# A Strassen-type down-projection reordered, with raw weights loaded by quadrants, the last norm on VectorE, and gate weights of two precisions in one tile

## Chip, cores and metric

One Trainium2 chip, one core. The metric is the time on the device of one launch, in microseconds. The kernel before takes 1428.85 us (median of three runs, 1427.64 to 1430.25).

## The reference

One layer of a hybrid decoder in float32: 1024 prompt tokens and 64 sample tokens (1088 rows together), width 1024. A norm, one input projection, a retention group and an mLSTM group, an output projection with norm and residual, then a feed-forward part with a causal convolution. What matters here, cut:

```
gates = h @ w_in[:, last 8 columns] + b_g         # input and forget gate of 4 heads
...
up   = rmsnorm(x, pre_ffn_g) @ w_up                # 1024 -> 2 * 2816
conv = sum(padded[:, j:j+L] * conv_w[j] for j in range(3)) + conv_b
ffn  = (gelu(conv[..., :2816]) * conv[..., 2816:]) @ w_down      # 2816 -> 1024
x    = x + rmsnorm(ffn, post_ffn_g)
```

## The kernel before

Activations lie transposed, features on partitions, tokens in four blocks of Q = 272 columns. A float32 product is made of three fp32r matmuls: both operands are split into a high part (a ScalarE copy) and a low part (a VectorE subtraction), and high x high, high x low, low x high are summed in PSUM. The program's instructions are ordered per engine by a scheduler ahead of time; an instruction that is ready in its model may stand in a queue before one that comes earlier in the code. `tc.issue_after` puts an instruction behind a given one of the same engine.

The gate projection (`gate_proj`, L281) uses one padded weight tile in which 4 of the first 32 columns are forget gates and 4 of the next 32 are input gates; `dense` (L153) makes 8 x 3 matmuls for each of four blocks, and two VectorE products with `rb` take the result from PSUM (L303, L304).

The down-projection is one level of a Strassen-Winograd scheme: seven products (`SEQ`, L1035) in place of eight, each over KH = 11 pairs of 128 input features, on 512 weight columns and 544 tokens. Weight quadrants A11, A21 are the two halves of one 512 KB row block of `w_down`, A12 and A22 those of the next; GpSimd forms S1 to S4 from them in place (L1074, tile `wd`). The matching activation operands B11 ... T4 were written to HBM (`bd`) by the up-projection and are loaded again per step (tile `rb`, L1083). `prep` (L1076) makes one step: load, split of the weight (`ra`, L1053 and L1054), split of the activations. `ready` keeps eight steps ahead of TensorE. A raw weight tile takes the place of an up-projection operand, so its loads wait for that operand's last matmul.

`mm` (L1111, tile `dn`) issues three matmuls of 272 columns; eight PSUM banks hold a product's 2 x 4 outputs. `evac` (L1136) adds them to four output blocks `facc`, two halves of four slices each; `sumsq` (L1126) squares a finished slice (ScalarE), adds it to the block's sum (VectorE, tile `facc_sq`) and applies the gain (ScalarE). In the last product, S4 x B22, the two token halves follow each other, 132 matmuls each, and between them the finished blocks are normed: `norm_rows` sums over partitions with a matmul by ones (L185) and makes the reciprocal root (L186 to L191), `write` multiplies (L1194), adds the residual `x1r` (L1195) and stores. The block sums of squares that are still missing at the start of that product are made in its second step (`half_square`).

```
todo = {0: lambda: [load_x1(b) for b in range(2)], 1: lambda: (half_square(), load_x1(2), load_x1(3)),
        3: lambda: norm_rows(0), 4: lambda: write(0), 5: lambda: norm_rows(1)}
...
todo = {0: lambda: write(1), 2: lambda: (norm_rows(2), write(2)), 3: lambda: (norm_rows(3), write(3))}
```

The first set stands behind the steps of the first half, the second behind the four groups of 33 matmuls of the second half.

Of the kernel before, what the change touches and what calls it, by code (L numbers as in the profile page):

```python
# [16 lines left out]
P = 128  # L17
# [75 lines left out]
def hybrid_layer_kernel(ctx: ExitStack, tc: tile.TileContext, a: dict, o: dict):  # L93
# [86 lines left out]
    def rstd_block(ssq, out, l, r, name, after=None):  # L180

        n = out.shape[1]
        ps = bank(psB, n, f"ssqb_{name}")
        with tc.issue_after(after.ins) if after else nullcontext():
            nc.tensor.matmul(ps, ones, ssq, start=True, stop=True)  # L185
        nc.vector.tensor_scalar(out, ps, 1.0 / D, EPS, ALU.mult, ALU.add)  # L186
        nc.scalar.activation(l, ps, AF.Ln, scale=1.0 / D, bias=eps)
        nc.scalar.activation(r, l, AF.Exp, scale=-0.5)
        nc.scalar.activation(l, r, AF.Square)
        nc.vector.scalar_tensor_tensor(l, l, -0.5, out, ALU.mult, ALU.mult)  # L190
        nc.vector.scalar_tensor_tensor(out, l, 1.5, r, ALU.add, ALU.mult)  # L191
# [92 lines left out]
    def gate_proj():  # L284
        xst = m2.tile([P, X_SEL], F32, tag="vx", bufs=1, name="xst")
        nc.sync.dma_start(xst, a["cx"][:, :X_SEL])
        xsel = m2.tile([P, X_N - X_SEL], F32, tag="sb", bufs=1, name="xsel")
        nc.sync.dma_start(xsel, a["cx"][:, X_SEL:])
        nc.vector.tensor_copy(idb, ident)
        nc.vector.tensor_copy(negb, xst[:, X_NEG:X_NEG + P])  # L290
        for t in vts:
            nc.gpsimd.memset(t[:, :, P:P + 1], 1.0)
        nc.vector.tensor_copy(negsb, xst[:, X_NEGS:X_NEGS + TS])
        nc.scalar.activation(sel, xsel[:100, :].rearrange("p (j h c) -> p j h c", j=2, h=NH), AF.Copy)
        fg = tok("fg", NH)
        ig = yT[3][:NH, 0, :]
        gates.extend([fg, ig])
        w = load_w(a["wg"], "gates")
        for b in range(4):
            o0, n = BLK[b]  # L300
            ps = bank(psA, n, f"gates{b}")
            dense(ps, w, h, b)
            nc.vector.tensor_tensor(fg[:, o0:o0 + n], ps[0:NH, :], rb[0:NH, o0:o0 + n], ALU.mult)  # L303
            nc.vector.tensor_tensor(ig[:, o0:o0 + n], ps[32:32 + NH, :], rb[32:32 + NH, o0:o0 + n], ALU.mult)  # L304
        nc.scalar.activation(fg, fg, AF.Identity, bias=vec[0:NH, V_BG:V_BG + 1])
        nc.scalar.activation(ig, ig, AF.Identity, bias=vec[0:NH, V_BG + 1:V_BG + 2])

# [724 lines left out]

    nc.sync.dma_start(o["conv"], cache.rearrange("p j s t -> p (j s t)"))
    log_exp_tables(last["gelu"])
    SEQ = (("A11", "B11"), ("A12", "B21"), ("A22", "T4"), ("S2", "T2"), ("S1", "T1"), ("S3", "T3"), ("S4", "B22"))  # L1035

    PLACE = {"A11": 0, "A21": 512, "A12": 1024, "A22": 1536, "S1": 0, "S3": 512, "S4": 1024, "S2": 1536}
# [13 lines left out]
    def halves(x, hi, lo):  # L1051
# [3 lines left out]
        return hi, lo  # L1055

    A, B, late = {}, {}, []
    sums_of = {1: ("S3", "A11", "A21", ALU.subtract), 2: ("S2", "A22", "S3", ALU.subtract),
               3: ("S1", "S2", "A11", ALU.add), 4: ("S4", "A12", "S2", ALU.subtract)}

    def prep_a(q, p):
        name = SEQ[q][0]
        if q < 2:
            nc.sync.dma_start(raw[p][:, q * D:(q + 1) * D], a["wd"][2 * p + q])
        if q == LAST and p > 7:
            if p % 2 == 0:
                late.append(slot(SLOTS[len(late)], f"ra_late{p}").rearrange("p k n -> p (k n)"))
            t = late[-1][:, p % 2 * D:(p % 2 + 1) * D]
        else:
            t = ring_a[(q * KH + p) % 8]  # L1070
        A[q, p] = halves(quad(p, name), t[:, :512], t[:, 512:])
        if q in sums_of:
            out, x, y, op = sums_of[q]
            nc.gpsimd.tensor_tensor(quad(p, out), quad(p, x), quad(p, y), op)  # L1074

    def prep(n):  # L1076

        q, p = divmod(n, KH) if n < LAST * KH else (LAST, 0)
        t = ring_b[n % 8]
        hi, lo = t[:, :HB], t[:, HB:]  # L1080
        if q < LAST:
            o0 = BD[SEQ[q][1]]
            nc.sync.dma_start(lo.bitcast(F32), bd[p][:, o0:o0 + HB])  # L1083
            prep_a(q, p)
            B[q, p] = halves(lo.bitcast(F32), hi, lo)
            return
        i, p = divmod(n - LAST * KH, 6)
        ps = range(2 * p, min(2 * p + 2, KH))
        o0 = BD["B22"] + i * Q
# [33 lines left out]
    acc = [t_acc[b // 2][:, b % 2 * Q:(b % 2 + 1) * Q] for b in range(4)]  # L1123
    begun = set()

    def sumsq(b, m, final=None):  # L1126

        t = facc[b][:, m, :]
        sq = acc[b] if b not in begun else t_acc[b // 2][:, 2 * Q:]
        nc.scalar.activation(sq, t, AF.Square)  # L1130
        if b in begun:
            nc.vector.tensor_tensor(acc[b], acc[b], sq, ALU.add)  # L1132
        begun.add(b)
        nc.scalar.activation(t, t, AF.Copy, scale=vec[:, V_POSTFFN + m:V_POSTFFN + m + 1])
# [161 lines left out]
```

## Time and profile before

| | |
|---|---|
| median of three runs | 1428.85 us |
| the profiled execution | 1428.44 us, span 1426.7 us |
| TensorE busy | 1361.6 us, 95% |
| VectorE busy | 1060.2 us, 74% |
| ScalarE busy | 587.0 us, 41% |
| GpSimd busy | 436.4 us, 31% |
| read from HBM, written | 97.88 MB, 35.50 MB |
| first down-projection matmul, last one | starts at 1152.27, at 1407.85 |

Times of rows are from the start of the span. Matmuls are pipelined, so a busy TensorE isn't one at its peak: look at the distance of starts, and at the granted clock. An idle stretch is put down to what released it.

### The profile page before, as it was taken

The page shows a single profiled execution, that of the slowest core. Times are in us where ns is not written, and L with a number is a line of the kernel's source. Part 1 is how long each engine was busy: PE and PEld are TensorE (multiplying, and loading weights), DVE is VectorE, ACT ScalarE, POOL GpSimd, SP SyncE. Part 2 cuts the span into 40 slices and gives each one's busy share as a digit, 9 for nine tenths or more (in the row PEclk, how much of TensorE's full clock was granted, in tenths as well). Part 3 has the DMA queues.
Part 4 walks back from the last instruction along what each step waited for, and adds up shares of the span by engine and source line. Part 5 has one row for each costly group of instructions (what it writes and reads, how often), then busy time and mean ns, then how long its engine had stood idle before and what let it go on. Part 6 is the DMA issues. An engine that isn't in the chain of part 4 may idle for free. (4 is left out here: it accounts for less than half of the span.)

```text
span 1426.7 us, 26779 instructions
## 1 busy us (share of the span) xinstructions
PE 1361.6 (95%) x10575; PEld 1332.3 (93%) x10575; DVE 1060.2 (74%) x2064; ACT 587.0 (41%) x1162; POOL 436.4 (31%) x433
## 2 busy tenths in 40 slices
PE   7999999999999999999998999999999979999993
PEld 7899999999999998999998999999999979999993
DVE  7845875455455466568899999999989995995577
ACT  6423542323223236445553433433433444454462
POOL 5200000001001000004456466465465460952015
PEclk9999999999999999999999999999999989999997
DMA  6112111121121113323022223322223394333352
GB/s 233 60 45 73 41 59 54 53 62 48 45 62 47 45 47 112 113 63 122 32 92 87 89 88 112 107 85 84 99 85 115 116 404 121 95 91 93 97 197 114
DMA packets 64478, 135.12 MB, mean 95 GB/s; under 512 B 6112, under 2 KB 30688, under 8 KB 63840
## 3 DMA queue, kind: packets, MB, share of 16 engines
q1 hardware_dynamic: 64352, 133.41, 27.6%
q8 instruction: 83, 1.36, 0.4%
q14 instruction: 43, 0.35, 0.1%
HBM read 97.88 MB, written 35.50 MB: 93 GB/s over the span
## 5 line engine op out<-in xcount | busy, mean ns | idle before, releaser
L159 PE MATMUL in<-hh,wh_in 128*128 128x272 f32 x1024 | 301.8, 295 | 11.1 <-ACT hh L198 6.8
L161 PE MATMUL in<-hh,wl_in 128*128 128x272 f32 x1024 | 301.1, 294 | 1.1 <-DVE wl_in L147 1.1
L160 PE MATMUL in<-hl,wh_in 128*128 128x272 f32 x1024 | 299.8, 293 | 1.2 <-DVE hl L199 1.2
L159 PEld LDWEIGHTS in<-hh,wh_in 128*128 128x128 f32 x1024 | 195.4, 191 | 12.9 <-ACT hh L198 6.8
L161 PEld LDWEIGHTS in<-hh,wl_in 128*128 128x128 f32 x1024 | 194.9, 190 | 3.7 <-issue 2.1
L160 PEld LDWEIGHTS in<-hl,wh_in 128*128 128x128 f32 x1024 | 195.4, 191 | 2.4 <-DVE hl L199 1.5
L147 DVE TENSOR_TENSOR wl_up<-st_up,wh_up 128x512 fp32r<-128x512 f32 x128 | 125.4, 985 | 9.5 <-ACT wh_up L145 9.4
L145 ACT ACTIVATE wh_up<-st_up 128x512 fp32r<-128x512 f32 x128 | 75.1, 620 | 133.1 <-POOL st_up L866 120.4
L1054 DVE TENSOR_TENSOR rb<-rb 128x544 fp32r<-128x544 f32 x78 | 73.1, 949 | 42.4 <-ACT rb L1053 42.2
L943 DVE SCALAR_TENSOR_TENSOR c<-Ug,vec,c 128x1024 f32<-128x1024 f32 x88 | 79.4, 939 | 9.5 <-ACT c L941 9.5
L1074 POOL TENSOR_TENSOR wd<-wd 128x512 f32<-128x512 f32 x44 | 72.0, 1667 | 42.7 <-DVE ra_dhi L1054 33.1
L943 DVE SCALAR_TENSOR_TENSOR c<-Uv,vec,c 128x1024 f32<-128x1024 f32 (+1 forms) x88 | 71.9, 822 | 9.3 <-ACT c L941 9.3
L958 POOL TENSOR_TENSOR act<-act 128x544 f32<-128x544 f32 x44 | 72.4, 1645 | 14.7 <-DVE act L950 10.3
L1053 ACT ACTIVATE rb<-rb 128x544 fp32r<-128x544 f32 x78 | 49.8, 648 | 64.3 <-DMA rb<-bd 58.4
L613 POOL TENSOR_TENSOR vx_r<-vts,cst 64x1024 f32<-64x1024 f32 x4 | 7.6, 1901 | 191.8 <-ACT vts L527 191.8
L902 DVE TENSOR_TENSOR Uv<-Uv,up_S 128x272 f32<-128x272 f32 (+1 forms) x200 | 63.5, 369 | 0.0
L941 ACT ACTIVATE c<-Ug,vec 128x1024 f32<-128x1024 f32 (+1 forms) x44 | 34.6, 835 | 67.0 <-DVE Ug L906 59.3
L145 ACT ACTIVATE wh_in<-st_in 128x1024 fp32r<-128x1024 f32 x32 | 33.9, 1059 | 62.3 <-PE in L160 58.3
L893 POOL MEMSET Ug<- 128x2 f32 x22 | 2.2, 100 | 176.9 <-DVE xr L791 82.1
L859 POOL TENSOR_TENSOR s<-st_up 128x512 f32<-128x512 f32 x20 | 29.0, 1450 | 85.2 <-DMA st_up<-in_wu 82.1
L613 POOL TENSOR_TENSOR vx_m<-vts,cst 64x1032 f32<-64x1032 f32 x4 | 7.7, 1914 | 152.6 <-DVE pt_m L559 152.6
L928 PE MATMUL up_A<-T4h,wh_up 128*128 128x272 f32 x160 | 47.9, 299 | 4.8 <-DVE Uv L902 4.7
(547 smaller groups left out, 4825.1 us busy)
## 6 DMA issues: line engine op xcount, KB each, us to landing
st_up<-in_wu SPq DMA_DIRECT2D x44, 512.0 KB, 3.3
rb<-bd SPq DMA_DIRECT2D x76, 272.0 KB, 2.8
bd<-act SPq DMA_DIRECT2D x33, 544.0 KB, 2.7
st_in<-in_wi SPq DMA_DIRECT2D x32, 512.0 KB, 3.3
wd<-in_wd SPq DMA_DIRECT2D x22, 512.0 KB, 9.3
x<-in_x SPq DMA_DIRECT2D x16, 272.0 KB, 7.0
xr<-in_x SPq DMA_DIRECT2D x8, 544.0 KB, 3.7
x1d<-mo SPq DMA_DIRECT2D x8, 544.0 KB, 3.1
```

The costliest lines, as they stand in the source:

```text
L145: nc.scalar.activation(hi, x, AF.Copy)
L147: eng.tensor_tensor(lo, x, hi.bitcast(F32), ALU.subtract)
L159: nc.tensor.matmul(ps, hi[:, ws], xh, start=k == 0, stop=False)
L160: nc.tensor.matmul(ps, hi[:, ws], xl, start=False, stop=False)
L161: nc.tensor.matmul(ps, lo[:, ws], xh, start=False, stop=k == KT - 1)
L902: nc.vector.tensor_tensor(o_, o_ if x is None else c(x), c(ps), ALU.add)
L928: nc.tensor.matmul(ps, wh[:, c], xh[:, k, n], start=k == 0, stop=False)
L943: nc.vector.scalar_tensor_tensor(c, u(i), cw(i), c, ALU.mult, ALU.add)
L958: nc.gpsimd.tensor_tensor(o_, x, y, ALU.subtract)
L1053: nc.scalar.activation(hi, x, AF.Copy)
L1054: nc.vector.tensor_tensor(lo, x, hi.bitcast(F32), ALU.subtract)
L1074: nc.gpsimd.tensor_tensor(quad(p, out), quad(p, x), quad(p, y), op)
```

## The change

The gate weights' high and low parts are put side by side in one tile of 128 columns, so two matmuls (by the high and the low activations) give four partial products; the lower 64 rows of PSUM are copied by ScalarE and added to the upper 64 by VectorE. In the down-projection, product A22 x T4 moves from third to last, S3, S2, S1 follow earlier in that order, and the sums S are formed in the step that uses them (S2 now in the place of S3). Raw weights are loaded as four quadrants of 256 KB: A11, A12, A22 with products 0, 1, 2, and A21 from the seventh step on. With A22 x T4 last, the first half of that product completes block 0 and the second block 1; blocks 2 and 3 are complete before it. The final multiplication and addition of `write` run on VectorE alone. The last square of block 1 isn't added to the sum: a second ones matmul adds it in PSUM. The last block is written in 4, 3 and 1 slices.

```diff
@@ rstd_block
-            nc.tensor.matmul(ps, ones, ssq, start=True, stop=True)
+            for i, x in enumerate(ssq if type(ssq) is list else [ssq]):
+                nc.tensor.matmul(ps, ones, x, start=i == 0, stop=type(ssq) is not list or i == len(ssq) - 1)
@@ gate_proj
-        w = load_w(a["wg"], "gates")
+        st = stage_w(a["wg"], "gates").rearrange("p (k c) -> p k c", k=KT)
+        w = wp.tile([P, D], F32R, tag="whi", name="w_gates").rearrange("p (k c) -> p k c", k=KT)
+        split_to(st[:, :, :64], w[:, :, :64], w[:, :, 64:])
...
-            dense(ps, w, h, b)
-            nc.vector.tensor_tensor(fg[:, o0:o0 + n], ps[0:NH, :], rb[0:NH, o0:o0 + n], ALU.mult)
-            nc.vector.tensor_tensor(ig[:, o0:o0 + n], ps[32:32 + NH, :], rb[32:32 + NH, o0:o0 + n], ALU.mult)
+            for k in range(KT):
+                for i, x in enumerate(h[b // 2][k // 4]):
+                    nc.tensor.matmul(ps, w[:, k, :], x[:, k % 4, qcols(b)], start=k == i == 0,
+                                     stop=k == KT - 1 and i == 1)
+            gs = m2.tile([P, Q], F32, tag="sw", name=f"gs{b}")[:64, :n]
+            nc.scalar.activation(gs, ps[64:, :], AF.Copy)
+            nc.vector.tensor_tensor(gs, gs, ps[:64, :], ALU.add)
+            nc.vector.tensor_tensor(fg[:, o0:o0 + n], gs[0:NH, :], rb[0:NH, o0:o0 + n], ALU.mult)
+            nc.vector.tensor_tensor(ig[:, o0:o0 + n], gs[32:32 + NH, :], rb[32:32 + NH, o0:o0 + n], ALU.mult)
@@ down-projection
-    SEQ = (("A11", "B11"), ("A12", "B21"), ("A22", "T4"), ("S2", "T2"), ("S1", "T1"), ("S3", "T3"), ("S4", "B22"))
+    SEQ = (("A11", "B11"), ("A12", "B21"), ("S3", "T3"), ("S2", "T2"), ("S1", "T1"), ("S4", "B22"), ("A22", "T4"))
-    PLACE = {..., "S1": 0, "S3": 512, "S4": 1024, "S2": 1536}
+    PLACE = {..., "S1": 0, "S3": 512, "S4": 1024, "S2": 512}
-    sums_of = {1: ("S3", ...), 2: ("S2", ...), 3: ("S1", ...), 4: ("S4", ...)}
+    sums_of = {2: ("S3", ...), 3: ("S2", ...), 4: ("S1", ...), 5: ("S4", ...)}
+    def load_quad(name, p):
+        c = PLACE[name] % D
+        nc.sync.dma_start(quad(p, name), a["wd"][2 * p + PLACE[name] // D, :, c:c + 512])
@@ prep_a
-        if q < 2:
-            nc.sync.dma_start(raw[p][:, q * D:(q + 1) * D], a["wd"][2 * p + q])
+        if q < 3:
+            load_quad(("A11", "A12", "A22")[q], p)
+        if 0 <= q * KH + p - 6 < KH:
+            load_quad("A21", q * KH + p - 6)
+        if q in sums_of:                          # moved up from behind the split
+            out, x, y, op = sums_of[q]
+            nc.gpsimd.tensor_tensor(quad(p, out), quad(p, x), quad(p, y), op)
@@ sumsq
-        if b in begun:
+        if apart:
+            acc[b] = [acc[b], sq]
+        elif b in begun:
             nc.vector.tensor_tensor(acc[b], acc[b], sq, ALU.add)
@@ evac
-        o_, x = ((c11, c22), None, (c22, c22), (c12, c22), (c22, c12), (c12, c12))[q - 1]
+        o_, x = ((c11, c22), None, (c22, c22), (c12, c22), (c12, c12), (c21, c21))[q - 1]
...
+        if q == 4:
+            nc.vector.tensor_tensor(c22, c21, t, ALU.add)
+            sumsq(2 + i, 4 + m)
         if q == 5:
-            nc.vector.tensor_tensor(c21, c21, t, ALU.add)
-            sumsq(i, 4 + m)
+            sumsq(2 + i, m)
         if q == 6:
-            sumsq(2 + i, m)
+            sumsq(i, 4 + m, (i, m) == (1, 3))
@@ write
-        for k0, k1 in ((0, 3), (3, 6), (6, 8)):
+        for k0, k1 in ((0, 4), (4, 7), (7, 8)) if b == 1 else ((0, 3), (3, 6), (6, 8)):
             t = facc[b][:, k0:k1, :]
-            mul = nc.gpsimd if b == 3 and k0 == 6 else nc.vector
-            add = nc.vector if b == 3 and k0 < 6 else nc.gpsimd
-            mul.tensor_tensor(t, t, r.unsqueeze(1).broadcast_to([P, k1 - k0, n]), ALU.mult)
-            add.tensor_tensor(t, t, x1[b][:, k0:k1, :], ALU.add)
+            nc.vector.tensor_tensor(t, t, r.unsqueeze(1).broadcast_to([P, k1 - k0, n]), ALU.mult)
+            nc.vector.tensor_tensor(t, t, x1[b][:, k0:k1, :], ALU.add)
             nc.sync.dma_start(yo[:, k0:k1, :], t)
@@ last product, first half, then second half
-    todo = {0: lambda: [load_x1(b) for b in range(2)], 1: lambda: (half_square(), load_x1(2), load_x1(3)),
-            3: lambda: norm_rows(0), 4: lambda: write(0), 5: lambda: norm_rows(1)}
+    todo = {0: lambda: [load_x1(b) for b in (2, 3, 0, 1)], 2: lambda: norm_rows(2), 3: lambda: write(2),
+            4: lambda: norm_rows(3)}
...
-    todo = {0: lambda: write(1), 2: lambda: (norm_rows(2), write(2)), 3: lambda: (norm_rows(3), write(3))}
+    todo = {0: lambda: write(3), 1: lambda: norm_rows(0), 2: lambda: write(0), 3: lambda: (norm_rows(1), write(1))}
```

## Rows read from the trace of the kernel before

**Rows 1.** Busy time by stretch: PE, PEld, DVE, ACT, POOL; clock, DMA share, GB/s
```profile
100.00:200.00 100.00, 96.98 (x739) 92.10 (x739) 71.81 (x195) 43.24 (x87) 4.96 (x5) 0.98 0.17 53
```

**Rows 2.** The same, at the start of the down-projection:
```profile
1155.00:1160.00 5.00, 2.99 (x15) 2.67 (x15) 5.00 (x8) 1.27 (x3) 4.21 (x5) 0.72 1.03 414
```

**Rows 3.** Timeline of product 0: start, duration, line; idle before and releaser in brackets
```profile
1152.27 0.29 PE L1118 MATMUL dn<-rb,ra_whi 128*128 128x272 f32 x1
...
1199.10 0.40 ACT L1140 ACTIVATE facc<-dn 128x272 f32<-128x272 f32 x1 [0.36 <-PE dn L1120]
```

**Rows 4.** Timeline of TensorE, fifteen dn matmuls in a row, first and last:
```profile
1381.33 0.29 PE L1118 MATMUL dn<-rb,ra_late 128*128 128x272 f32 x1
...
1383.08 0.29 PE L1120 MATMUL dn<-rb,ra_late 128*128 128x272 f32 x1
```

**Rows 5.** TensorE's waits, 1130 to 1250: total us, times, longest
```profile
PE dn L1118 <- DVE Uv L902: 4.4, 3, 2.6
PE dn L1118 <- ACT rb L1053: 2.2, 1, 2.2
...
PE dn L1119 <- DVE rb L1054: 1.5, 1, 1.5
```

**Rows 6.** Timeline of TensorE at the end of the last product:
```profile
1395.92 0.29 PE L1120 MATMUL dn<-rb,ra_late 128*128 128x272 f32 x1
1400.69 1.27 PE L185 MATMUL ssqb_fin<-facc_sq,ones 128*128 128x272 f32 x2 [4.48 <-DVE facc_sq L1132]
1401.37 0.81 PE L1118 MATMUL dn<-rb,ra_whi 128*128 128x272 f32 x1
...
1407.85 0.29 PE L1120 MATMUL dn<-rb,ra_late 128*128 128x272 f32 x1
```

**Rows 7.** Busy time by stretch, the last 33 dn matmuls:
```profile
1401.30:1408.20 6.90, 6.84 (x35) 6.50 (x33) 5.03 (x9) 3.30 (x8) 1.13 (x2) 0.63 0.25 94
```

**Rows 8.** Timeline of VectorE at the end:
```profile
1406.45 4.27 DVE L1194 TENSOR_TENSOR facc<-facc,fin 128x816 f32<-128x816 f32 x3
1410.65 0.42 DVE L1143 TENSOR_TENSOR facc<-facc,dn 128x272 f32<-128x272 f32 x1
1411.57 1.23 DVE L1132 TENSOR_TENSOR facc_sq<-facc_sq 128x272 f32<-128x272 f32 x1 [0.49 <-ACT facc_sq L1130]
...
1416.70 3.06 DVE L1194 TENSOR_TENSOR facc<-facc,fin 128x816 f32<-128x816 f32 x2
1419.68 3.05 DVE L1195 TENSOR_TENSOR facc<-facc,x1r 128x816 f32<-128x816 f32 x2
```

**Rows 9.** VectorE by line: duration in ns, least, median, most:
```profile
L1132 DVE TENSOR_TENSOR facc_sq<-facc_sq x28: 426/438/2174, 1235.5 to 1411.6; 128x272 f32<-128x272 f32 x28
L1143 DVE TENSOR_TENSOR facc<-facc,dn x40: 422/427/439, 1232.1 to 1410.7; 128x272 f32<-128x272 f32 x40
L1195 DVE TENSOR_TENSOR facc<-facc,x1r x2: 995/1562/2129, 1419.7 to 1421.7; 128x816 f32<-128x816 f32 x2
L1054 DVE TENSOR_TENSOR rb<-rb x78: 430/725/1871, 1139.2 to 1381.2; 128x544 fp32r<-128x544 f32 x76, 128x272 fp32r<-128x272 f32 x2
```

**Rows 10.** The gates' tile, one of its three matmul groups:
```profile
L161 PE MATMUL gates<-hh,wl_gates x32: 282/288/391, 122.5 to 143.6; 128*128 128x272 f32 x32
```

**Rows 11.** The raw weights' tile, its load issues:
```profile
L1064 SPq DMA_DIRECT2D wd<-in_wd x22: 327/332/806, 1137.5 to 1164.2; - x22
```

**Rows 12.** Timeline of SP's queue, two groups of issues:
```profile
1151.28 8.18 SPq L1064 DMA_DIRECT2D wd<-in_wd  x8
1160.41 1.56 SPq L1083 DMA_DIRECT2D rb<-bd  x2
```

**Rows 13.** Tile rb, its loads:
```profile
DMA to landing us min/median/max: 2.0/2.8/9.2
```

**Rows 14.** DMA issues of the page: KB each, median us to landing
```profile
st_up<-in_wu SPq DMA_DIRECT2D x44, 512.0 KB, 3.3
```

**Rows 15.** Busy time by stretch, loads of x at the kernel's start:
```profile
10.00:14.00 4.00, 4.00 (x20) 4.00 (x20) 4.00 (x8) 3.81 (x9) 1.72 (x3) 1.00 1.03 412
```

More of the change, by code (lines that the diff above doesn't have):

```diff
@@ L1034, in hybrid_layer_kernel @@
     log_exp_tables(last["gelu"])
-    SEQ = (("A11", "B11"), ("A12", "B21"), ("A22", "T4"), ("S2", "T2"), ("S1", "T1"), ("S3", "T3"), ("S4", "B22"))
-    PLACE = {"A11": 0, "A21": 512, "A12": 1024, "A22": 1536, "S1": 0, "S3": 512, "S4": 1024, "S2": 1536}
+    SEQ = (("A11", "B11"), ("A12", "B21"), ("S3", "T3"), ("S2", "T2"), ("S1", "T1"), ("S4", "B22"), ("A22", "T4"))
+    PLACE = {"A11": 0, "A21": 512, "A12": 1024, "A22": 1536, "S1": 0, "S3": 512, "S4": 1024, "S2": 512}
     LAST = len(SEQ) - 1
@@ L1057, in hybrid_layer_kernel @@
     A, B, late = {}, {}, []
-    sums_of = {1: ("S3", "A11", "A21", ALU.subtract), 2: ("S2", "A22", "S3", ALU.subtract),
-               3: ("S1", "S2", "A11", ALU.add), 4: ("S4", "A12", "S2", ALU.subtract)}
+    sums_of = {2: ("S3", "A11", "A21", ALU.subtract), 3: ("S2", "A22", "S3", ALU.subtract),
+               4: ("S1", "S2", "A11", ALU.add), 5: ("S4", "A12", "S2", ALU.subtract)}
+    def load_quad(name, p):
+        c = PLACE[name] % D
+        nc.sync.dma_start(quad(p, name), a["wd"][2 * p + PLACE[name] // D, :, c:c + 512])
     def prep_a(q, p):
         name = SEQ[q][0]
-        if q < 2:
-            nc.sync.dma_start(raw[p][:, q * D:(q + 1) * D], a["wd"][2 * p + q])
+        if q < 3:
[5 more added lines that the diff above has]
+            nc.gpsimd.tensor_tensor(quad(p, out), quad(p, x), quad(p, y), op)
         if q == LAST and p > 7:
@@ L1071, in prep_a @@
         A[q, p] = halves(quad(p, name), t[:, :512], t[:, 512:])
-        if q in sums_of:
-            out, x, y, op = sums_of[q]
-            nc.gpsimd.tensor_tensor(quad(p, out), quad(p, x), quad(p, y), op)
     def prep(n):
@@ L1088, in prep @@
         ps = range(2 * p, min(2 * p + 2, KH))
-        o0 = BD["B22"] + i * Q
+        o0 = BD[SEQ[LAST][1]] + i * Q
         m = len(ps) * Q
@@ L1124, in hybrid_layer_kernel, with sumsq @@
     begun = set()
-    def sumsq(b, m, final=None):
+    def sumsq(b, m, apart=False):
         t = facc[b][:, m, :]
@@ L1139, in evac @@
         if q in (0, 2):
-            nc.scalar.activation((c22, c11, c21)[q], t, AF.Copy)
+            nc.scalar.activation((c22, None, c21)[q], t, AF.Copy)
             return
-        o_, x = ((c11, c22), None, (c22, c22), (c12, c22), (c22, c12), (c12, c12))[q - 1]
+        o_, x = ((c11, c22), None, (c22, c22), (c12, c22), (c12, c12), (c21, c21))[q - 1]
         nc.vector.tensor_tensor(o_, x, t, ALU.add)
@@ L1170, in hybrid_layer_kernel @@
             ready((q + 1) * KH + 2)
-    x1, fin = [], []
+    x1, fin = {}, {}
     def load_x1(b):
-        x1.append(slot(SLOTS[2 + b], f"x1r_{b}", F32).rearrange("p k n -> p (k n)").rearrange("p (k n) -> p k n", k=KT))
+        x1[b] = slot(SLOTS[2 + b], f"x1r_{b}", F32).rearrange("p k n -> p (k n)").rearrange("p (k n) -> p k n", k=KT)
         nc.sync.dma_start(x1[b], x1cols(b))
@@ L1179, in load_x1 @@
             t = slot(SLOTS[6 + b // 2], f"fin{b}", F32).rearrange("p k n -> p (k n)")
-            fin.extend((t[:, 2 * i * Q:(2 * i + 1) * Q], t[:, (2 * i + 1) * Q:2 * (i + 1) * Q]) for i in range(2))
+            for i in range(2):
+                fin[b + i] = t[:, 2 * i * Q:(2 * i + 1) * Q], t[:, (2 * i + 1) * Q:2 * (i + 1) * Q]
     def norm_rows(b):
-        rstd_block(acc[b], *fin[b], acc[b], f"fin{b}", last["dn"] if b < 3 else None)
+        rstd_block(acc[b], *fin[b], acc[b][0] if b == 1 else acc[b], f"fin{b}", last["dn"] if b != 1 else None)
     def write(b):
@@ L1189, in write @@
         yo = o["y"][:, KT * o0:KT * (o0 + n)].rearrange("p (k n) -> p k n", k=KT)
-        for k0, k1 in ((0, 3), (3, 6), (6, 8)):
+        for k0, k1 in ((0, 4), (4, 7), (7, 8)) if b == 1 else ((0, 3), (3, 6), (6, 8)):
             t = facc[b][:, k0:k1, :]
-            mul = nc.gpsimd if b == 3 and k0 == 6 else nc.vector
-            add = nc.vector if b == 3 and k0 < 6 else nc.gpsimd
-            mul.tensor_tensor(t, t, r.unsqueeze(1).broadcast_to([P, k1 - k0, n]), ALU.mult)
-            add.tensor_tensor(t, t, x1[b][:, k0:k1, :], ALU.add)
+            nc.vector.tensor_tensor(t, t, r.unsqueeze(1).broadcast_to([P, k1 - k0, n]), ALU.mult)
+            nc.vector.tensor_tensor(t, t, x1[b][:, k0:k1, :], ALU.add)
             nc.sync.dma_start(yo[:, k0:k1, :], t)
-    def half_square():
-        for i, m in grid:
-            sumsq(2 + i, 4 + m)
-    todo = {0: lambda: [load_x1(b) for b in range(2)], 1: lambda: (half_square(), load_x1(2), load_x1(3)),
-            3: lambda: norm_rows(0), 4: lambda: write(0), 5: lambda: norm_rows(1)}
+    todo = {0: lambda: [load_x1(b) for b in (2, 3, 0, 1)], 2: lambda: norm_rows(2), 3: lambda: write(2),
+            4: lambda: norm_rows(3)}
     for t in range(6):
```

## Prediction

> **What bounds the kernel now.** I read four views, from the whole to the place. First the busy times by stage. In the stage of the gate projection TensorE is busy for 97 of 100 us [rows 1], so a matmul that is left out there comes off the end, as long as nothing later is fixed in time; all later work follows TensorE's. Then the same view in slices of 5 us over the start of the down-projection: TensorE is busy for 2.99 of 5 us and runs at a granted clock of 0.72, part of the time at 1.2 GHz, while the DMA engines are full (a share of 1.03, 414 GB/s) and VectorE is busy all 5 us [rows 2]. Product 0 of the down-projection begins at 1152.27; its seventh bank of eight is copied out, straight after its last matmul, at 1199.10 [rows 3]. With 0.75 us for the eighth (six matmuls at 0.125 us each, 14 steps in 1.75 us [rows 4]), that is 47.6 us for 264 matmuls that need 33.0. So 14.6 us are lost. The list of waits says to whom: 4.4 us to VectorE, which clears PSUM (Uv L902), and 2.2 and 1.5 us to operands that a transfer brought late (rb) [rows 5]; the rest is matmuls at the lower clock and short gaps.
>
> Third, the end. The ones matmul of the third final norm stands in TensorE's queue ahead of the last 33 matmuls and waits 4.48 us for VectorE's sum of squares: dn matmuls stop at 1395.92 and start again at 1401.37 [rows 6], after the idle time at a granted clock of 0.63 for the stretch [rows 7], so 1.2 GHz for most of it and 2.4 at its end, and 33 of them then take 6.6 us instead of 4.1. Lost: 5.3 + 2.5 = 7.8 us. Last, the chain behind the final matmul (start 1407.85): VectorE still multiplies block 2 (4.27 us from 1406.45), so the last evacuation starts at 1410.65, 2.5 us after the matmul's end; then a sum of 1.23 us, the norm, two products (3.06 us) and two sums (3.05 us) [rows 8].
>
> VectorE is slow there because GpSimd adds the residual at the same time. The same 128x272 sum of two SBUF operands takes 0.43 us at best and 2.17 at worst; one with a PSUM operand stays at 0.43 to 0.44 throughout [rows 9].
>
> **The change, part by part.** The profiled execution took 1428.44 us, a span of 1426.7 and 1.7 around it; the median of the runs is 1428.85, 0.4 above. I sum against 1428.44 and add 0.4.
>
> *Gates.* 96 matmuls become 64: a third of them (x32 of L161 [rows 10]) go. 32 x 0.125 = 4.0 us off. Added: a ScalarE copy and a VectorE sum for each of four blocks, 4 x 0.43 = 1.7 us on VectorE, less half of one weight split. A bank was held for two VectorE products from PSUM, of the length of the sums from PSUM, 0.43 each [rows 9]; now for a copy and a sum of about that length: no change for TensorE. Cover: TensorE's own queue of projections; without it, 1.7 us. Bounds 4.0 and 2.3. I take 4.0.
>
> *Raw weights by quadrants.* 22 loads of 512 KB become 44 of 256 KB. Only A11 is needed in product 0; A12 in product 1, A21 and A22 in product 2. But order in the code isn't order in the queue: before, all 22 were issued from 1137.5 to 1164.2 [rows 11], though 11 belong to product 1, because each goes as soon as its slot is free. Eight of them filled 8.2 us of SP's queue, and the two rb loads behind them went at 1160.41 [rows 12]; an rb load lands in 2.8 us, the worst in 9.2 [rows 13], and the chain of waits runs through this one. With halves, the queue holds half as many bytes at any depth, and A11 goes ahead of the rest. Upper bound of the gain: all 14.6 us. Lower bound: nothing, if all 44 are drawn forward and the same 11.5 MB stand ahead of rb. Nearest rows: TensorE's own waits for rb, 2.2 + 1.5 = 3.7 us [rows 5]. I take 3.7; the waits for Uv I leave, since VectorE's load there (weight halves, convolution, with GpSimd's S3 sums beside them) has the same instructions.
>
> The price of smaller loads: an rb load of 272 KB lands in 2.8 us [rows 13], one of 512 KB in 3.3 [rows 14], so alone, a half is dearer by the byte. The Trainium skill (DMA: Bandwidth & Descriptors, sections Anatomy of one DMA and Bandwidth) speaks against this edit: it has a fixed part of about 2 us in each transfer, measured on GpSimd's path, and asks for 1 MiB or more for 75% of peak; taken one by one, 22 more loads would come to 44 us by that page, an estimate. The trace disagrees where loads overlap: with 272 KB loads of x in flight the engines move 412 GB/s at 10 to 14 us [rows 15]. So I charge nothing for rate; 22 more issues of 0.33 us [rows 11] are 7 us of SP's queue spread over three products.
>
> *Order of products, sums.* The S sums on GpSimd are the same 44, each now in the step that uses it; they still run when their inputs are there, eight steps ahead. Product 4 gets a second evacuation sum and the squares of block 2+i: 24 VectorE operations of 0.43 busy (0.35 from start to start) = 8.4 us, within about 12 us that TensorE takes to return to its eighth bank, beside 1.4 us of weight and operand splits for each 3 us, 5.6 us there. That is 14 against 12, and splits run eight steps ahead: nothing, at worst 2 us. In return the eight squares leave product 6.
>
> *The end.* Blocks 2 and 3 are now complete before product 6, their norms stand in its first half, where their sums are long done. In the second half only the norm of block 0 stands in TensorE's queue, 8.3 us in (two of four groups of 33 matmuls); behind it wait the last 66. It needs four squares, which go one by one through one buffer: a square, a sum and, in between, one operation of a write. On VectorE alone 816 columns take 0.995 us and 544 columns 0.725 [rows 9], so a write is 4 x 0.995 + 2 x 0.725 = 5.4 us. Four rounds of 0.43 + 0.43 + 1.0 = 1.9 us, begun about 1 us into the half, end 8.6 us in: about even. I allow a wait of 1.0 us and 0.4 for the norm's own matmul: 7.8 - 1.4 = 6.4 us off. Bounds: 7.4 off and 0 (the old wait comes back).
>
> VectorE's work in the second half is write 3 and write 0 (10.8), seven evacuations with their sums (5), two norms (2.6): 18.4 us against 16.5 of matmuls. So the last evacuation waits some 2 us as before; nothing gained. Then the sum of 1.23 us goes (its place is taken by a second ones matmul, 0.2 to 0.4 us, behind the first), and the write of 4, 3 and 1 slices of 272 is 2 x 1.28 + 2 x 0.995 + 2 x 0.43 = 5.4 us instead of 6.1 (1088 columns at 1.28 by the line through 272 and 816), with a smaller last transfer: 0.9 + 0.7 + 0.3 = about 2 us; with half of the late start taken back at most, 2.5. I take 2.5, bounds 0 and 4.5.
>
> **Sum:** 4.0 + 3.7 + 6.4 + 2.5 = 16.6 us off 1428.4, 1411.8; as a median, 1412.
>
> **The rivals.**
>
> *A, the loads are not spread* (0.2): all 44 are issued as early as the 22 were; for it: the 11 early ones of product 1 [rows 11]. Product 0 loses what it lost. 12.9 us off: 1416.
>
> *B, the start is freed entirely* (0.15): the transfers' relief also moves GpSimd's S3 sums out of the time in which VectorE clears PSUM, and the clock stays up. For it: a split of 544 columns takes 0.725 us as a rule and up to 1.87 beside GpSimd [rows 9]. Against it: the same instructions. 14.6 instead of 3.7: 1401.
>
> *C, VectorE becomes the bound at the end* (0.14): it takes over all residual sums, and by the count above has 18.4 us of work for 16.5. If the writes stand ahead of block 0's sums, the norm's matmul waits as it did: the 6.4 go, and of the 2.5 about 2. 4.0 + 3.7 + 0.5 = 8 us off: 1420.
>
> *D, slower* (0.07): the 44 loads hold SP's queue. Eight went in 8.2 us, 1.02 each [rows 12]; if a half holds it as long, 22 more take 22.5 us, and the rb loads of product 0 stand behind them. The other parts give 12.9, so 22.5 makes 1438; it decides from 12.9 us on. Against it: the 1.02 us are the time that 400 GB/s need for most of 512 KB, and a half needs half. By the Trainium skill's rule above (DMA: Bandwidth & Descriptors, Anatomy of one DMA) this is the way it would go; the rows at 10 to 14 us don't bear it out.
>
> **How the numbers follow.** The forecast has 0.44; it is a sum of four terms that lie in different stages, so three must fail for no gain. 0.2%, 2.9 us, is about what a measurement here can tell from no change. Faster: the forecast, A, B and most of C, 0.89. Within: 0.04, a C with a part of D. Slower: D, 0.07. The range reaches from B to C: 1401.5 to 1420.5; outside lie D, the tails of B and the slower part of C, some 2 in 10. The forecast's own is 1407 to 1416.
>
> **What would show it.** Gates: 64 matmuls, and TensorE's work 4 us earlier behind them. Start: product 0 from first matmul to last evacuation 44 us instead of 47.6, no wait of TensorE for rb; rb's time to landing in this stretch below 9 us. End: no gap above 1.5 us in dn matmuls and a full granted clock to the last; final sum gone, and about 16 us from last matmul to the end, against 18.9 from the start of the last one. Wrong if: rb lands as late as before (A), the ones matmul of block 0 waits over 3 us (C), or SP's queue spends over 1 us on each quadrant (D).

## The result, and the profile after

The changed kernel takes 1419.31 us (median of four runs, 1417.52 to 1421.65), the kernel before in the same comparison 1428.76: a ratio of 0.9934, 95% interval 0.9917 to 0.9951, 9.5 us faster. That lies inside the range, 7 us above the forecast, outside the forecast's own 1407 to 1416, and near the figure of rival C (1420). The profiled execution took 1419.54, a span of 1417.8.

Where the 8.9 us of the span came from, by the starts of matmuls (a product has 264 of them, counted off along TensorE's timeline; each row of a product gives the start of its first one):

| starts at | before | after | gained so far | in this stretch |
|---|---|---|---|---|
| last matmul of the input projection | 552.2 | 548.1 | 4.1 | 4.1 |
| first dn matmul (product 0) | 1152.3 | 1151.8 | 0.5 | -3.6 |
| product 1 | 1199.6 | 1198.7 | 1.0 | 0.5 |
| product 2 | 1232.7 | 1231.7 | 1.0 | 0 |
| product 3 | 1267.2 | 1265.3 | 1.8 | 0.8 |
| product 6 | 1366.2 | 1364.4 | 1.8 | 0 |
| last dn matmul | 1407.9 | 1403.9 | 4.0 | 2.2 |
| end of the span | 1426.7 | 1417.8 | 8.9 | 4.9 |

So of the 4.1 us at the end of the input projection 0.5 were left when the down-projection began. Its product 0 gave 0.5, product 2 gave 0.8, and the end (product 6 and what follows it) gave 7.1.

TensorE's waits from 1130 to 1250, after (total us, times, longest), against [rows 5]:

```profile
PE dn L1133 <- DVE Uv L911: 5.1, 2, 2.9
PE up_A L937 <- DVE Uv L911: 2.1, 2, 1.5
PE dn L1133 <- ACT rb L1062: 1.7, 1, 1.7
PE dn L1133 <- DVE Ug L915: 1.4, 2, 0.9
```

One wait for rb stays (1.7 us where there were 2.2 and 1.5), and the waits for VectorE, which clears Uv and Ug, are longer. SP's queue in that stretch, against [rows 11, 12]:

```profile
1138.38 4.12 SPq L1072 DMA_DIRECT2D wd<-in_wd  x8
...
1143.52 5.24 SPq L1072 DMA_DIRECT2D wd<-in_wd  x7
...
1150.16 6.03 SPq L1072 DMA_DIRECT2D wd<-in_wd  x10
1156.59 0.97 SPq L1098 DMA_DIRECT2D rb<-bd  x2
...
1173.75 0.33 SPq L1072 DMA_DIRECT2D wd<-in_wd  x1
```

All 44 quadrants are drawn forward, as rival A had it, the last at 1173.75; in the groups shown a quadrant holds the queue for 0.52 to 0.75 us (4.12 / 8 to 5.24 / 7), not for 1.02 as rival D needed.

The end. TensorE's timeline, against [rows 6], and the same stretch by busy time and granted clock (the last three columns are clock, DMA share, GB/s):

```profile
1389.97 0.29 PE L1135 MATMUL dn<-rb,ra_late 128*128 128x272 f32 x1
1393.86 1.27 PE L186 MATMUL ssqb_fin<-facc_sq,ones 128*128 128x272 f32 x2 [3.61 <-DVE facc_sq L1149]
1394.55 0.81 PE L1133 MATMUL dn<-rb,ra_whi 128*128 128x272 f32 x1
...
1403.87 0.29 PE L1135 MATMUL dn<-rb,ra_late 128*128 128x272 f32 x1
```

```profile
1389.90:1396.80 6.90, 3.29 (x14) 2.84 (x14) 5.14 (x10) 3.44 (x8) 0.00 (x0) 0.75 0.43 165
```

The ones matmul of block 0 waits 3.61 us for the sum of squares, dn matmuls pause for 4.6 us, and the clock is 0.75 in that stretch. VectorE's timeline says why, and shows the tail (against [rows 8]):

```profile
1387.37 0.44 DVE L1149 TENSOR_TENSOR facc_sq<-facc_sq 128x272 f32<-128x272 f32 x1
1387.72 2.56 DVE L1212 TENSOR_TENSOR facc<-facc,fin 128x816 f32<-128x816 f32 x3
1390.19 0.44 DVE L1149 TENSOR_TENSOR facc_sq<-facc_sq 128x272 f32<-128x272 f32 x1
1390.55 1.93 DVE L1213 TENSOR_TENSOR facc<-facc,x1r 128x816 f32<-128x816 f32 x2
...
1393.36 0.44 DVE L1149 TENSOR_TENSOR facc_sq<-facc_sq 128x272 f32<-128x272 f32 x1
...
1404.20 0.44 DVE L1160 TENSOR_TENSOR facc<-facc,dn 128x272 f32<-128x272 f32 x1 [0.16 <-PE dn L1135]
...
1408.79 2.56 DVE L1212 TENSOR_TENSOR facc<-facc,fin 128x1088 f32<-128x1088 f32 x3
1411.27 2.56 DVE L1213 TENSOR_TENSOR facc<-facc,x1r 128x1088 f32<-128x1088 f32 x3
```

Between the second, third and fourth sum of block 0 (L1149) stands the write of block 3 (L1212, L1213). Behind the last matmul VectorE is free at once (0.16 us), the sum of 1.23 us is gone, and product and residual take 5.1 us instead of 6.1.

### The profile page after: what moved, and what is told of

It is laid out like the page before. It is cut to its first block, busy times and chain, and to the rows that moved or that the text cites. A ratio compares the mean times of both kernels' runs of the same rounds, so it can differ in the third digit from the quotient of the medians.

```text
span 1417.8 us, 26731 instructions
## 1 busy us (share of the span) xinstructions
PE 1356.5 (96%) x10545; PEld 1327.1 (94%) x10545; DVE 1053.8 (74%) x2078; ACT 589.8 (42%) x1166; POOL 412.2 (29%) x422
## 5 line engine op out<-in xcount | busy, mean ns | idle before, releaser
L147 DVE TENSOR_TENSOR wl_up<-st_up,wh_up 128x512 fp32r<-128x512 f32 x128 | 121.1, 951 | 13.5 <-ACT wh_up L145 13.3
L1063 DVE TENSOR_TENSOR rb<-rb 128x544 fp32r<-128x544 f32 x78 | 68.5, 890 | 39.1 <-ACT rb L1062 38.7
L1133 PE MATMUL dn<-rb,ra_whi 128*128 128x272 f32 x152 | 46.2, 304 | 6.4 <-DVE Uv L911 5.1
```

What stands on the lines that cost most here:

```text
L147: eng.tensor_tensor(lo, x, hi.bitcast(F32), ALU.subtract)
L1063: nc.vector.tensor_tensor(lo, x, hi.bitcast(F32), ALU.subtract)
L1133: nc.tensor.matmul(t, wh[:, ms], ah, start=k == 0, stop=False)
```

## The experiments

Twelve kernels ran. The ratio is to the kernel before, with its interval; "dn", "product 1" and "last" are starts of dn matmuls in the profile, "tail" goes from the last one to the end of the span. The kernel before was timed again beside each group of runs, so a difference of two ratios can be set beside that of two medians. In the kernels whose start is the same (the changed one, e3, e4, e8) product 0 takes 46.3 to 47.9 us: so much do single profiles differ.

| run | median us | ratio | dn | product 1 | last | tail |
|---|---|---|---|---|---|---|
| before | 1427 to 1428.8 | 1 | 1152.3 | 1199.6 | 1407.9 | 18.8 |
| after | 1419.31 | 0.9934 [0.9917, 0.9951] | 1151.8 | 1198.7 | 1403.9 | 13.9 |
| e1 gates alone | 1426.85 | 0.9989 [0.9980, 0.9999] | 1148.9 | 1196.4 | 1402.7 | 20.2 |
| e2 whole rows | 1421.24 | 0.9956 [0.9943, 0.9968] | 1152.5 | 1201.3 | 1406.3 | 14.2 |
| e3 GpSimd adds | 1422.76 | 0.9973 [0.9958, 0.9988] | 1151.9 | 1198.2 | 1406.5 | 14.8 |
| e4 write 3 later | 1415.83 | 0.9917 [0.9904, 0.9931] | 1150.6 | 1198.5 | 1398.3 | 15.8 |
| e5 A21 late | 1406.84 | 0.9858 [0.9845, 0.9872] | 1149.9 | 1189.3 | 1390.3 | 15.7 |
| e6 A12, A22 late | 1411.88 | 0.9894 [0.9879, 0.9909] | 1153.7 | 1193.4 | 1394.0 | 15.8 |
| e7 all in step | 1411.08 | 0.9885 [0.9871, 0.9898] | 1150.9 | 1188.3 | 1394.2 | 15.8 |
| e8 old gates | 1419.57 | 0.9950 [0.9938, 0.9963] | 1151.3 | 1198.2 | 1403.7 | 14.1 |
| e9 sums late | 1411.28 | 0.9887 [0.9873, 0.9900] | 1149.1 | 1192.7 | 1393.8 | 15.7 |
| e10 tail | 1405.39 | 0.9842 [0.9828, 0.9855] | 1150.8 | 1188.2 | 1390.2 | 14.1 |
| e11 old gates in e10 | 1406.23 | 0.9847 [0.9832, 0.9861] | 1149.8 | 1189.8 | 1391.0 | 14.1 |
| e12 before, sums late | 1422.64 | 0.9960 [0.9947, 0.9974] | 1150.1 | 1194.5 | 1402.6 | 18.5 |

**The gates (e1, e8, e11).** e1 is the kernel before with the new `gate_proj`; e8 and e11 put the old one into the changed kernel and into e10.

> The kernel before with the changed gate projection and nothing else. Theory 1 (given back on the way): the input projection ends 4 us earlier, but the up-projection, where VectorE and GpSimd are nearly always busy and get in each other's way, gives most of it back, as in the changed kernel, where 4.1 us at 548 us are 0.5 us at the first dn matmul; 0 to 1.5 us off the end. Rival (the forecast's step): the 4 us arrive, first dn matmul at about 1148 instead of 1152, 1424.8 us in all, and what the changed kernel lost in the up-projection is due to something else in the change, or is chance.

> The changed kernel with the old gate projection (96 matmuls). Theory 1 (the up-projection gives most of a 4 us shift back): 0 to 2 us slower than the changed kernel's 1419.3. Rival (the shift arrives, and the loss in the runs so far is chance): 4 us slower, 1423.3.

> The kernel of the tail experiment (1405.4) with the old gate projection of 96 matmuls. In six kernels so far with the short gates the middle one was 1.0 to 2.4 us later, counted from the end of the input projection to the multiplication of the twentieth pair of the up-projection, than the two with 96 matmuls. Theory 1 (that loss comes with the short gates each time, and the rest of what was lost at the start of the down-projection is gone here): 1.5 to 2.5 us slower, 1407 to 1408, and that stretch 570.5 to 571 us as in the other two, instead of 571.9 to 572.8. Rival (the 4 us arrive once the start is cleared): 4 us slower, 1409.4. Second rival (the stretch varies from run to run whatever the gates): it lies above 571.5 us here too.

Measured: the short gates gain 1.1, 0.3 and 0.8 us by the medians, 1.6, 2.3 and 0.7 by the ratios (e8 against the changed kernel, e11 against e10; the intervals of these pairs overlap). The 4 us don't arrive; about 1 us does. e11 fell below its own theory's 1.5 to 2.5. That e1's first dn matmul starts at 1148.9, near the rival's 1148, doesn't speak for the rival: e1's profile is of one of its faster executions (1424.69), and of the 3.4 us 2.1 were there at the first gates matmul (120.0 against 122.2). The profiles show two of the places where the rest goes. TensorE's waits in the input projection, and the stretch behind the gates by busy time and clock, first in e11 (long gates), then in e10 (short):

```profile
PE in L159 <- DVE k_r L432: 1.8, 1, 1.8
...
PE in L159 <- DVE q_r L432: 1.2, 1, 1.2
150.00:200.00 50.00, 46.98 (x363) 44.19 (x361) 47.10 (x110) 25.85 (x52) 3.03 (x4) 1.00 0.13 41
```

```profile
PE x_r L524 <- DVE k_r L442: 2.9, 1, 2.9
...
PE in L159 <- DVE q_r L440: 0.7, 1, 0.7
150.00:200.00 50.00, 46.40 (x346) 43.48 (x345) 45.33 (x114) 25.19 (x51) 3.80 (x4) 0.97 0.15 48
```

With the short gates TensorE comes earlier to the keys that VectorE is still rotating and waits 2.9 us in one piece instead of 1.8 (3.6 in all instead of 3.0). From the first gates matmul to the end of the input projection it takes 426.5 us in e10 instead of 428.5 in e8, e11 and e12: 2.0 us gained. The granted clock of 0.97 over 50 us, against 1.00, would be 1.5 us by itself, but it isn't what took the other 2.0. In e1, e2 and e3, also with short gates, the clock is 1.00 there, TensorE waits in a third place, and the stretch takes 426.1 us. In e1:

```profile
PE o_r L661 <- DVE S_r L665: 0.3, 1, 0.3
150.00:200.00 50.00, 45.95 (x350) 42.53 (x349) 45.87 (x113) 22.77 (x48) 3.25 (x4) 1.00 0.17 55
```

So at the same clock the short gates gain 2.4 of 4.0 us; 1.1 of the rest are longer waits for VectorE (4.1 us in e1, 3.0 in e11), and 0.5 are in gaps too short for the list. The kernel before took 430.0, with a clock of 0.97 of its own in its profiled execution; that, and 0.5 us from ahead of the gates, made the gain look like 4.1.

More goes in the output and up-projection. From the end of the input projection to the multiplication of the twentieth pair, the four kernels with long gates (before, e8, e11, e12) take 570.5, 570.8, 571.0 and 571.1 us, the ten with short gates 571.9 to 572.8: 0.8 to 2.4 us, with no overlap, while the instructions of the up-projection stand in the same order on every engine. From 645 to 765 us GpSimd's instructions in the changed kernel come 3.1 us earlier than before, to 0.02 us, but for two that start at the landing of a transfer and end in step again. At 765.6 a third does so, 2.4 us earlier, and the step isn't found again: from then on VectorE's operations beside GpSimd are stretched at other places. Why the sum comes out on the same side ten times is open. VectorE is nearly full there, busy for 458 of the 500 us from 640 to 1140 in the changed kernel; GpSimd, with 272, isn't, against what e1's theory took.

**Quadrants against whole rows (e2).** The edit, from the changed kernel:

```diff
-        if q < 3:
-            load_quad(("A11", "A12", "A22")[q], p)
-        if 0 <= q * KH + p - 6 < KH:
-            load_quad("A21", q * KH + p - 6)
+        if q < 2:
+            nc.sync.dma_start(raw[p][:, q * D:(q + 1) * D], a["wd"][2 * p + q])
```

> The changed kernel with the raw weights loaded as 22 whole rows of 512 KB (with products 0 and 1), as before; all else as changed. Theory 2 (the quadrants are worth nothing: VectorE sets the pace of product 0, and all loads are drawn forward in either form): within 1.5 us of the changed kernel's 1419.3. Rival (the forecast's step): TensorE waits for rb again, 3.7 us slower, 1423.

Measured: 1.9 us slower than the changed kernel by the medians, 3.1 by the ratios, whose intervals overlap; product 0 takes 48.8 us, and 46.3 to 47.9 in the kernels with the changed kernel's start. TensorE's waits at the start in e2:

```profile
PE dn L1131 <- DVE Uv L911: 4.2, 3, 2.4
PE dn L1131 <- ACT rb L1062: 2.2, 1, 2.2
PE dn L1132 <- DVE rb L1063: 1.6, 1, 1.6
```

The two waits for rb of [rows 5] come back. So inside the new order the quadrants seem to earn 1 to 3 us, by what the forecast named. That lies between theory 2's bound of 1.5 and the rival's 3.7, and the noise leaves both open. Against the kernel before, whose product 0 takes 47.4 us, the changed kernel's 46.9 hardly shows it.

**GpSimd's residual sums (e3).** The cut edit; the slices of the last block's write and its last product also go back to what they were:

```diff
-            nc.vector.tensor_tensor(t, t, x1[b][:, k0:k1, :], ALU.add)
+            add = nc.vector if b == 1 and k0 < 6 else nc.gpsimd
+            add.tensor_tensor(t, t, x1[b][:, k0:k1, :], ALU.add)
```

> The changed kernel with the residual sums of the final writes on GpSimd again (and the first two of the last block on VectorE, its last product on GpSimd, slices 3, 3, 2), as before; order of products as changed. Theory 3 (the gain of 7.2 us behind the start of the last product comes from VectorE alone: its operations are stretched while GpSimd adds): nearly all of it goes, 5 to 7 us slower than the changed kernel, 1424 to 1426, the ones matmul of block 0 waits over 4.5 us and the last evacuation starts 2 us or more after the last matmul. Rival (the new order of products brings it, since blocks 2 and 3 are complete earlier): at most 1.5 us slower, 1421.

Measured: 3.4 us slower by the medians, 5.6 by the ratios. GpSimd's and VectorE's timelines in e3, and TensorE's wait:

```profile
1389.33 4.61 POOL L1215 TENSOR_TENSOR facc<-facc,x1r 128x816 f32<-128x816 f32 x2 [3.37 <-ACT facc L1151]
```

```profile
1390.03 2.14 DVE L1149 TENSOR_TENSOR facc_sq<-facc_sq 128x272 f32<-128x272 f32 x1
1392.09 2.42 DVE L1214 TENSOR_TENSOR facc<-facc,fin 128x544 f32<-128x544 f32 x1
1394.44 0.42 DVE L1160 TENSOR_TENSOR facc<-facc,dn 128x272 f32<-128x272 f32 x1
```

```profile
PE ssqb_fin L186 <- DVE facc_sq L1149: 7.0, 2, 6.5
```

A sum of 0.44 us takes 2.14 beside GpSimd, the evacuation from PSUM stays at 0.42, and the ones matmul waits 6.5 us. The stall is theory 3's, and product 6 takes 42.6 us instead of 39.5. The last evacuation isn't late after such a stall, against theory 3, and the tail of 14.8 us keeps most of its gain against 18.8.

**The write of block 3 behind block 0's sums (e4).** The cut edit:

```diff
-    todo = {0: lambda: write(3), 1: lambda: norm_rows(0),
+    sum0 = last["sum"]                 # last sum of squares of block 0
+    def write_3():
+        with tc.issue_after(sum0.ins):
+            write(3)
+    todo = {0: write_3, 1: lambda: norm_rows(0),
```

> The changed kernel with the write of block 3 put behind the last sum of squares of block 0 on VectorE. Theory 4 (the 3.6 us that TensorE waits in the last product come from that write standing between the four sums, which share one buffer for the square): no wait of the ones matmul of block 0, full clock to the end, 5 to 6 us off, 1413.5 to 1414.5. Rival (VectorE has more work in the second half than TensorE has matmuls, the forecast's 18.4 against 16.5 us): the wait goes and comes back behind the last matmul, where VectorE is still in the write of block 0; 0 to 2 us off, 1417.5 to 1419.3.

Measured: 3.5 us faster by the medians, 2.4 by the ratios, whose intervals overlap. The last product by busy time and clock, and VectorE behind the last matmul (which starts at 1398.30):

```profile
1363.90:1398.50 34.60, 34.60 (x274) 34.36 (x273) 29.43 (x57) 19.70 (x44) 0.00 (x0) 1.00 0.39 133
```

```profile
1396.98 2.56 DVE L1212 TENSOR_TENSOR facc<-facc,fin 128x816 f32<-128x816 f32 x3
1399.46 0.43 DVE L1160 TENSOR_TENSOR facc<-facc,dn 128x272 f32<-128x272 f32 x1
1399.80 2.55 DVE L1213 TENSOR_TENSOR facc<-facc,x1r 128x816 f32<-128x816 f32 x3
1402.28 0.43 DVE L187 TENSOR_SCALAR fin<-ssqb_fin 128x272 f32<-128x272 f32 x1
```

TensorE is busy throughout at a clock of 1.00: the wait did come from that write. Product 6 takes 34.3 us instead of 39.5, the last matmul is 5.6 us earlier, and 1.9 us of it comes back in the tail, where the write of block 0 now stands ahead of the last evacuation and of the last norm. Both accounts hold, one after the other.

**The start of the down-projection (e5, e6, e7, e9, on e4; e12 on the kernel before).** e5 loads A21 with steps 14 to 24, e6 leaves A21 early and holds A12 and A22 in their steps, e7 does both, e9 and e12 leave every load and put only the S3 sums behind GpSimd's last work for the up-projection. The edits, cut and put together:

```diff
+        with tc.issue_after(last["rb"].ins):       # e5: A21; e6: A12 and A22; e7: all
             nc.sync.dma_start(quad(p, name), ...)
-        if 0 <= q * KH + p - 6 < KH:                # e5, e7
+        if 0 <= q * KH + p - 14 < KH:
+            with tc.issue_after(last["pool"].ins): # e9, e12 alone
                 nc.gpsimd.tensor_tensor(quad(p, out), quad(p, x), quad(p, y), op)
```

> The kernel of the last experiment (write of block 3 later), and in it the loads of A21 with steps 14 to 24, each behind that step's rb load in SP's queue: so GpSimd's eleven sums S3, which ran at 1143 to 1167, come behind its last work for the up-projection. A12 and A22 are still drawn forward, 33 loads in place of 44 in the first 35 us. Theory 5 (VectorE sets the pace at the start, slowed by GpSimd beside it): VectorE's splits of 512 columns at 1143 to 1170 fall from up to 1.8 us to about 0.7, product 0 from 46.8 to 48 us down to 42 to 44, 4 to 5 us off that kernel's 1415.8. Rival (the transfers set it): with 33 of 44 loads still in front, product 0 stays at 46 us or more, under 1.5 us off.

> The same base; here the loads of A12 and A22 stand behind the rb load of their step in SP's queue, and A21 with the eleven S3 sums is early, as in the changed kernel: 22 loads in the first 35 us instead of 44. Theory 5 (VectorE slowed by GpSimd): product 0 stays within 1 us of 47.5, the total within 1.5 us of 1415.8. Rival (the transfers set it): the waits for rb and for late weights go, product 0 falls to 44 us or less, 3 to 4 us off.

> The same base with both: every quadrant behind the rb load of its step, A21 with steps 14 to 24. Theory 5: as with A21 late alone, 4 to 5 us off 1415.8, and within 1 us of that run. Rival (the transfers): 3 to 4 us off, but as with A12 and A22 late alone. If both count, more than either, product 0 at 40 us or less, 1408 to 1409 in all.

> The kernel with the write of block 3 later (1415.8), and in it only the order of GpSimd changed: the eleven S3 sums stand behind its last work for the up-projection; all 44 loads are drawn forward as in the changed kernel. Theory 5 (GpSimd beside VectorE is the cost of the start): product 0 at 39 to 41 us and 7 to 9 us off, as with A21 loaded late (1406.8). Rival (the fewer loads, 33 for 44, did it there): product 0 at 45 us or more, under 3 us off.

> The kernel before with one edit: GpSimd's S3 sums behind its last work for the up-projection. Theory 5 (the 14.6 us lost in product 0 are mostly GpSimd's doing, and have nothing to do with quadrants): product 0 falls from 47.2 us to about 40, 6 to 8 us off the kernel before. Rival (whole rows of 512 KB hold the start): product 0 at 45 us or more, under 2 us off.

Measured, from e4's 1415.8 by the medians: e5 9.0 us faster, e6 4.0, e7 4.8, e9 4.6 (8.4, 3.3, 4.6 and 4.3 by the ratios); e12 is 5.2 faster than the kernel before. Product 0 takes 47.9 us in e4, 39.4 in e5, 39.8 in e6 (where it begins 3.1 us later), 37.4 in e7, 43.6 in e9, 44.4 in e12. GpSimd first: its S3 sums and VectorE's weight splits in the changed kernel, then such a split in e9, where GpSimd is idle at that time:

```profile
1151.38 1.78 DVE L1063 TENSOR_TENSOR ra_wlo<-wd,ra_wlo 128x512 fp32r<-128x512 f32 x1
1163.21 1.77 DVE L1063 TENSOR_TENSOR ra_dlo<-wd,ra_dlo 128x512 fp32r<-128x512 f32 x1
```

```profile
1151.30 1.30 POOL L1082 TENSOR_TENSOR wd<-wd 128x512 f32<-128x512 f32 x1 [0.41 <-DMA wd<-in_wd]
...
1159.27 8.08 POOL L1082 TENSOR_TENSOR wd<-wd 128x512 f32<-128x512 f32 x5
```

```profile
1157.39 0.68 DVE L1063 TENSOR_TENSOR ra_dlo<-wd,ra_dlo 128x512 fp32r<-128x512 f32 x1
```

1.78 us beside GpSimd, 0.68 without it: the difference, 1.1, is about one GpSimd sum (1.27 at least). The Trainium skill (SBUF — State Buffer, section SBUF: two separate sides) has it that VectorE, where it reads two operands from SBUF, and GpSimd exclude each other for a whole instruction; the trace agrees.

But e9 also shows the other half. Its chain of waits at 1172, and TensorE's timeline there:

```profile
1173.02 5.29 DMA rb<-bd
...
1178.40 0.67 ACT rb L1062
```

```profile
1179.11 1.78 PE L1134 MATMUL dn<-rb,ra_dlo 128*128 128x272 f32 x8 [3.69 <-ACT rb L1062]
```

Now that VectorE is quick, an rb load behind the 44 quadrants lands after 5.3 us and TensorE waits 3.7. e12, with whole rows, waits 4.6 in the same way. e5 takes away both: eleven loads fewer in front and no sums beside the first splits. TensorE waits for no operand of product 0 any more; two waits are left in it, for VectorE, which clears Uv and Ug:

```profile
PE dn L1134 <- DVE Uv L911: 2.1, 1, 2.1
PE dn L1134 <- DVE Ug L915: 1.1, 1, 1.1
```

So each theory was half right: the sums cost about 4.5 us, the early loads as much again. For e9 the rival's "under 3 us off" and theory 5's "7 to 9" both missed, and e12 falls between its two in the same way. e5 went past theory 5's 4 to 5, e6 met the rival's 3 to 4, and e7 stayed 2 us short of the 1408 to 1409 expected if both count. e7 gets the shortest product 0 and gives 4.0 us back at 1221, because its S3 sums, still waiting for A21, then run beside the splits of product 1 (VectorE and GpSimd in e7):

```profile
1221.49 1.78 DVE L1063 TENSOR_TENSOR rb<-rb 128x544 fp32r<-128x544 f32 x1
...
1224.86 1.12 DVE L1161 TENSOR_TENSOR facc<-facc,dn 128x272 f32<-128x272 f32 x3
```

```profile
1204.05 29.59 POOL L1083 TENSOR_TENSOR wd<-wd 128x512 f32<-128x512 f32 x18 [0.18 <-DMA wd<-in_wd]
```

**The tail (e10, on e5).** The edit, cut:

```diff
+    with tc.issue_after(last["evac"].ins):            # write of block 0: third product
+        nc.vector.tensor_tensor(t, t, r..., ALU.mult)
+    with tc.issue_after(last["mean" if k0 else "evac"].ins):   # its sums
+        nc.vector.tensor_tensor(t, t, x1[0][:, k0:k1, :], ALU.add)
```

> The kernel with A21 late (1406.8), and the write of block 0 laid around the last norm on VectorE: its third multiplication behind the last evacuation, its first sum behind that, its other two sums behind the first step of the last norm, where VectorE waits 1.5 us for ScalarE. Theory 6 (the tail of 15.6 us holds 0.8 us for a late evacuation and 1.2 us for sums ahead of the norm): 1.5 to 2 us off, 1405 in all, last matmul to end 14 us. Rival (the tail's length is that of the last norm, write and transfer): under 0.5 us.

Measured: 1.5 us off by the medians, 2.3 by the ratios, whose intervals overlap; tail 14.1 us instead of 15.7, as theory 6 had it. The chain of waits in e10:

```profile
1390.67 0.35 DVE facc L1161
...
1392.57 0.35 DVE fin L187
```

The last evacuation starts 0.5 us after the start of its last matmul, 1.0 in e5, and the norm's first step comes 1.9 us behind it, not 2.8. At 1405.39, a ratio of 0.9842 (0.9828 to 0.9855), e10 is the fastest: 13.9 us below the changed kernel by the medians.

## Why the prediction was right, and where its terms were not

- **Faster, and inside the range: right, in part by luck.** The forecast's 16.6 us became 8.9 in the span, and none of its four terms came out near its size: three were too large, the tail too small. The time is inside the range because that reached up to rival C, whose cause isn't the one that was found.
- **Gates, 4.0 off: mis-sized, about 1 measured.** The 32 matmuls went and TensorE ended the stage earlier, by 2.0 to 2.4 us. What failed is the step that named TensorE's own queue as the cover and let all later work follow it. In the input projection VectorE's rotation of keys came too late for the earlier TensorE (1.1 us more waiting at the same clock), and the output and up-projection took 0.8 to 2.4 us longer. Of the six figures from e1, e8 and e11 only one reaches the lower bound, 2.3.
- **Quadrants, 3.7 off: 0.5 measured in product 0.** The step "A11 goes ahead of the rest" failed: all 44 were issued by 1174, rival A. rb's landing did fall below 9 us (L1098: 5.9 at most), but a wait of 1.7 stayed and VectorE's grew. Inside the new order e2 finds 1 to 3 us for the quadrants. The step that left the waits for Uv, since VectorE's load there "has the same instructions", missed the larger share: those instructions were long because of GpSimd (e9, e12), which rival B had named and the forecast took as not moved. To charge nothing for the rate of small loads was nearly right: from 1138 to 1170 the engines move 371 GB/s instead of 396, and e2, with the large loads, still comes out the slower. By the Trainium skill's fixed part (DMA: Bandwidth & Descriptors, section Anatomy of one DMA) it would have been 44 us, an estimate; no run shows that.
- **Order of products: nothing forecast, 0.8 gained** in product 2, at whose start TensorE waits twice 0.4 us for facc before and once after. Product 4 takes 33.0 us before and after, so its added sums cost nothing, as forecast. No run takes the order alone.
- **The stall, 6.4 off: 2.2 measured.** The step that failed is "in between, one operation of a write": the static order put 2.5 us of products, and then 2.8 of sums with an evacuation, between the sums of block 0, so the wait is 3.6 us, not 1.0, and over the 3 that the prediction set as a sign of C. It is rival C's place and price, but not its cause: VectorE wasn't the bound, the order was, and e4 takes the wait away with the same work.
- **The tail, 2.5 off: 4.9 measured.** What failed is the step that lets the last evacuation wait some 2 us as before. VectorE was free for it (0.16 us idle), because TensorE's stall had let it catch up. e4 shows it from the other side: without the stall, 1.9 us come back here. Stall and tail together gave 7.1 us, and with the stall gone, in e4, 10.4 (41.7 - 34.3 in product 6 and 18.8 - 15.8); the forecast had 8.9 for both. No run takes the smaller last slices or the second ones matmul alone.

## What to carry to other kernels

Matmuls that are left out early are worth what arrives at the end. Waits for another engine soon behind them, and a later stage in which that engine is nearly full, can keep most of it: compare the starts of stages, not the end alone. Where VectorE's operations are two or three times their shortest length, look at what GpSimd does in those microseconds, and move that before anything else; a scheduler draws forward whatever has its inputs, so work and loads that aren't due need to be held back by name. When a wait is taken away, read which engine used it to catch up.

## What the runs showed of the hardware

- Loads of 256 KB, many in flight, move somewhat less than those of 512 KB at a full DMA share: 385 GB/s in the stretch from 1155 to 1160, against 414 before [rows 2]; from 1138 to 1170, 371 against 396, and 400 in e2.

```profile
1155.00:1160.00 5.00, 2.80 (x14) 2.37 (x13) 4.51 (x8) 3.55 (x7) 3.38 (x5) 0.78 1.05 385
```

- Two kernels with the same instructions (before and after, GpSimd from 645 to 765) keep their shift of 3.1 us to 0.02 us over 120 us; it changes where an instruction starts at the landing of a transfer.
- After a pause of 4.6 us dn matmuls start 0.23 us apart for about 2 us, which is the lower of the clock's two levels (1.2 GHz); without the pause (e4) the granted clock is 1.00 to the last dn matmul.
